# Layer 0's attention: two of three conditioning vectors as running sums on VectorE instead of products on TensorE

## The chip, the cores and the metric

The kernel runs on one core of a Trainium2 chip. The metric is the device time of one execution in microseconds (us), lower is better. TensorE (PE) multiplies, VectorE (DVE), ScalarE (ACT) and GpSimd (POOL) work element by element, SyncE (SP) issues the transfers from memory. Each engine runs its own instructions in the order in which they were written into its queue, and waits for the others through semaphores.

## The reference

A two-layer encoder over 512 positions of width 1024. Layer 0 mixes with pooling and attention, layer 1 with a matrix memory, and each layer ends with a gated channel mixer. Every sub-layer is scaled, shifted and gated by six vectors per layer, all computed from one conditioning vector `c`:

```
cond = jax.nn.silu(c)
for layer in range(DEPTH):
    mod = cond @ ada_w[layer] + ada_b[layer]
    sh1, sc1, g1, sh2, sc2, g2 = jnp.split(mod, 6, axis=-1)
    h = modulate(rms_norm(x), sh1, sc1)
    y = pool_attention_mixer(h, ...)          # layer 0
    x = x + g1[:, None, :] * y
    h = modulate(rms_norm(x), sh2, sc2)
    x = x + g2[:, None, :] * swiglu(h, ...)
```

Each of the six vectors is a product of a row of 1024 numbers with a 1024x1024 matrix: 4 MB of weights for 1024 results. Vectors 0 and 1 (`sh1`, `sc1`) are needed first, vector 2 (`g1`) when the mixer's output is added to `x`, vectors 3 and 4 (`sh2`, `sc2`) for the norm after that.

## The kernel before

Everything is held transposed, features on the 128 partitions and positions along the free dimension. Large products are done in three passes of split float32 (`p_hi*whi`, `p_lo*whi`, `p_hi*wlo`), so each weight slab is cast by ScalarE (`whi`, L116) and its remainder formed by VectorE (`wlo`, L120).

The stage of interest is layer 0's attention, in `even`. It runs `attend` twice, once for each half of the positions (hf 0, then hf 1), 16 units each. A unit is: two products give the scores (`psc`, L840 and L841), VectorE takes the row maximum (`nm`, L843, then a small multiply L846), ScalarE the exponential (`p`, L849), VectorE the reciprocal of its sum (`pr`, L851), GpSimd scales (`p`, L852), TensorE transposes four blocks (`ppt`, L862), ScalarE copies them out (`pt`), and after every second unit TensorE multiplies with the values (`pav`, L874). Between the units of hf 0 stand the last two blocks of the pooling input (`pu`), the four pooling windows (VectorE and GpSimd, `csum`, `win`, `pooled`) and the pooling products (`ppp`). Between those of hf 1 stands the output projection (`pout`, from `project`, woven in at four steps per unit); each of its output tiles is added into `x` by VectorE (`xT`, L332), which also frees the PSUM bank.

Two ways to compute a conditioning vector exist in the code. `ada_pe` streams the weights through TensorE: 16 products of a 32-column stationary with 512 columns per vector (`pada<-araw,silc`, four per tile of 1 MB), then a copy, four transposes (L84) and two small VectorE instructions (L279, L281). `ada` lets VectorE sum them: one scaled copy (`aacc<-araw,silc`, L245) and seven multiply-adds over 128x1024 (L247), a 32x32 block transpose in place (L253), a reduction (L255), four tiny products (`pada<-apart,fold`, L259) and one add (L262). Both read the same tiles `araw` through the same two buffers. Before the change, vectors 2, 3 and 4 of layer 0 go through `ada_pe` during hf 0, and the other seven through `ada` during the channel mixer of layer 0.

From this stage on, the order on each engine is not the order of the code: the compiler's scheduler places instructions by its own estimate of when each could run. The order is fixed in the program; at run time each engine follows its own.

Of the kernel before, what the change touches and what calls it, by code (L numbers as in the profile page):

```python
# [40 lines left out]
def weave(main, *others):  # L41

    for _ in main:
        for g, n in others:
            for _ in range(n):
                if next(g, StopIteration) is StopIteration:
                    break


def drain(g):  # L50
    for _ in g:
        pass


class Trunk:
# [502 lines left out]
    def even(self):  # L558
        nc, a, tc = self.nc, self.a, self.tc
        with ExitStack() as es:  # L560
            at = self.open(es, "at", 1)
            self.qst = self.b.tile([P, KD, S], F32R, name="qst", tag="B_hi")
            kv = self.b.tile([P, KD, S], F32R, name="kvst", tag="B_lo")
            self.kst = kv[:, 0:4]
            self.vst = at.tile([P, NTB, P], F32, name="vst")
            pooled = at.tile([P, 4, S], F32, name="pooled")
            self.edge = at.tile([P, 4, 16], F32, name="edge")
            nc.scalar.dma_start(self.edge, a["k_edge"].partition_broadcast(P))
            self.win = at.tile([P, S], F32, name="win")
            self.csum = at.tile([P, 529], F32, name="csum")  # L570
            nc.gpsimd.memset(self.csum[:, 0:9], 0.0)
            self.rq = [at.tile([P, 2 * NTB], F32, name=f"rq{b}") for b in range(4)]
            slab = None

            def u_block(g):
                nonlocal slab
                if g % 2 == 0:
                    slab = self.next_slab()
                ps = self.bank("pu")
                yield from self.gemm(ps, slab, g % 2, self.h, slice(0, S))  # L580
                if g % 2 == 1:
                    self.free_slabs()
                nc.scalar.copy(pooled[:, g], ps)

            with ExitStack() as es2:
                nt = self.open(es2, "nt", 1)
                self.rope = nt.tile([P, 2, S], F32, name="rope")
                self.load(self.rope, a["k_rope"])
                ada = self.ada_pe(2, 3, 4)
                next(ada)  # L590
                swap = nt.tile([P, P], F32, name="swap")
                i4, s4 = (t.rearrange("p (d t) -> p d t", t=2) for t in (self.ident, swap))
                for e in range(2):
                    nc.gpsimd.tensor_copy(s4[:, :, e:e + 1], i4[:, :, 1 - e:2 - e])
                us = (x for g in range(2) for x in u_block(g))

                def fill(n):
                    for _ in range(n):
                        next(us, None)

                k, v = self.rope_k(nt, swap), self.take_v(nt)
                q = [self.rope_q(nt, swap, b) for b in range(4)]
                for g, n in ((k, 1), (v, 1), (q[0], 1), (v, 1), (k, 1), (q[1], 1), (q[0], 2), (q[2], 2), (q[1], 2),
                             (q[3], 2), (q[2], 2), (q[3], 0)):
                    next(g)
                    fill(n)
                drain(us)
            self.chained = False
            self.mix = self.pair(self.keep, "A")
            self.banks(1)  # L610
            slabs = [None] * 4
            acc = self.square_sums("sqm")
            aw = self.open(es, "aw", 2)
            with tc.issue_after(self.split_ins.ins):
                pool = self.pool_project(pooled)
                next(pool)
                rest = (s for g in (2, 3) for s in u_block(g))
                for i, _ in enumerate(self.attend(aw, 0)):
                    with self.behind(self.sc_ins):
                        for _ in range(2 - i % 2):  # L620
                            next(rest, None)
                        if i < 16:
                            next(ada, None)
                    if i == 11:
                        drain(rest)
                        self.want(*[(a["w_eo"][s], "v") for s in (0, 1, 2, 3, 0)])
                        self.live = 1
                        self.load_slabs()
                    if i in WINDOW_STEPS:
                        with tc.issue_after(self.p_ins.ins), tc.issue_after(self.nm_ins.ins):  # L630
                            self.pool_window(WINDOW_STEPS.index(i), pooled)
                    if i >= POOL_STEP and i % 2 == 0:
                        next(pool, None)
                drain(pool)
            proj = self.project(0, slabs, range(4), self.mix, KD, 0, 2, acc[0])
            drain(ada)
            weave(self.attend(aw, 1), (proj, 4))
            drain(proj)
        self.ffn_want(0)
        self.h2 = self.pair(self.b, "B")  # L640
        self.close(0, slabs, self.mix, KD, 0, 2, acc, 3, self.h2)
        self.banks(0)
# [737 lines left out]
```

## Time and profile before

| | |
|---|---|
| time, median of 3 runs | 1214.58 us (1214.17 to 1219.38) |
| time of the profiled execution | 1214.87 us |
| its span, first to last instruction | 1213.1 us |
| TensorE busy | 1195.9 us, 99% of the span |
| VectorE busy | 656.3 us, 54% |
| ScalarE busy | 476.4 us, 39% |
| GpSimd busy | 135.2 us, 11% |
| mean granted TensorE clock | 0.999 |

Matmuls overlap one another, so a busy TensorE says that it had work, not that it ran at its peak. The chain of waits, followed back from the last instruction, is 92% TensorE.

### The profile page before, as it was taken

The numbers are of one execution on the slowest core, as the hardware profiler recorded it, in microseconds if no ns is written. First come the engines' busy times: TensorE is split into PE (matmuls) and PEld (weight loads), VectorE is DVE, ScalarE is ACT, GpSimd is POOL, SyncE is SP. The second block draws the span as 40 slices with busy tenths as digits, with TensorE's granted clock in tenths as the row PEclk, the third lists the DMA queues.
The fourth block names the chain that finished last, engine by engine and source line by source line (L and its number), as shares of the span: only waits on it lengthen the run. The fifth ranks groups of instructions, "written<-read, shape, count | busy, mean of one in ns | idle before, by whom it ended". The sixth has DMA issues, their size and how long they took to land.

```text
span 1213.1 us, 17266 instructions
## 1 busy us (share of the span) xinstructions
PE 1195.9 (99%) x6930; PEld 1020.9 (84%) x6930; DVE 656.3 (54%) x1111; ACT 476.4 (39%) x902; POOL 135.2 (11%) x151
## 2 busy tenths in 40 slices
PE   8999999999999999999899999999999999999998
PEld 6676689988888888889898999999888888888888
DVE  4576865574865677225878857556523323242233
ACT  4465764433213222223567757534423113221221
POOL 0033220011001110100000101100111001100110
PEclk9999999999999999999999999999999999999999
DMA  9605712274754565222624111113233223232232
GB/s 387 234 29 215 245 51 70 71 277 160 290 209 166 216 242 214 100 79 88 217 70 140 43 63 60 46 59 114 76 101 111 98 87 122 70 106 102 78 96 79
DMA packets 43168, 160.18 MB, mean 132 GB/s; under 512 B 4560, under 2 KB 11344, under 8 KB 36944
## 3 DMA queue, kind: packets, MB, share of 16 engines
q1 hardware_dynamic: 42240, 158.75, 37.2%
q8 instruction: 54, 0.88, 0.3%
q10 hardware_dynamic: 848, 0.33, 0.1%
q14 instruction: 26, 0.21, 0.1%
HBM read 154.87 MB, written 4.19 MB: 131 GB/s over the span
## 4 chain that ended last, share of the span: by engine, by line
PE 92%; DMA 3%; DVE 3%; ACT 1%; issue 1%; POOL 0%; SPq 0%; DVEq 0%; ACTq 0%; POOLq 0%
PE pf L78 53%; PE pout L78 10%; PE po L78 4%; PE pqk L78 3%; PE ppv L1210 3%; PE pv L78 3%; PE z L78 3%; PE pu L78 2%; DMA wraw<-in_w_dram 2%; PE pav L874 2%; PE pada L78 2%; PE ppt L862 1%; DMA wraw<-in_w_od_dram 1%; DVE wlo L120 1%; PE psc L840 1%
## 5 line engine op out<-in xcount | busy, mean ns | idle before, releaser
L78 PE MATMUL pf<-p_lo,whi 128*128 128x512 f32 (+1 forms) x1024 | 383.4, 376 | 0.9 <-DVE p_lo L366 0.9
L78 PE MATMUL pf<-p_hi,wlo 128*128 128x512 f32 (+1 forms) x1024 | 383.0, 376 | 0.0
L78 PE MATMUL pf<-p_hi,whi 128*128 128x512 f32 (+1 forms) x1024 | 380.8, 377 | 1.5 <-ACT p_hi L365 1.5
L116 ACT CAST whi<-wraw 128x1024 fp32r<-128x1024 f32 (+1 forms) x193 | 190.6, 1028 | 335.0 <-PE pf L78 234.8
L120 DVE TENSOR_TENSOR wlo<-wraw,whi 128x1024 fp32r<-128x1024 f32 (+1 forms) x193 | 229.7, 1223 | 137.8 <-ACT whi L116 134.8
L78 PEld LDWEIGHTS pf<-p_lo,whi 128*128 128x128 f32 x1024 | 192.7, 188 | 35.9 <-DVE p_lo L366 1.1
L78 PEld LDWEIGHTS pf<-p_hi,wlo 128*128 128x128 f32 x1024 | 192.5, 188 | 34.9
L78 PEld LDWEIGHTS pf<-p_hi,whi 128*128 128x128 f32 x1024 | 191.0, 188 | 36.6 <-ACT p_hi L365 1.9
L120 POOL TENSOR_TENSOR p_lo<-gf,p_hi 128x512 fp32r<-128x512 f32 (+1 forms) x48 | 70.6, 1474 | 580.3 <-ACT p_hi L116 580.3
L674 DVE TENSOR_TENSOR gf<-pf,si 128x512 f32<-128x512 f32 (+1 forms) x48 | 31.1, 647 | 161.2 <-PE pf L78 144.8
L78 PE MATMUL pout<-p_hi,whi 128*128 128x256 f32 x320 | 91.5, 287 | 0.3 <-DVE xT L332 0.3
L78 PE MATMUL pout<-p_lo,whi 128*128 128x256 f32 x320 | 90.8, 284 | 0.0
L78 PE MATMUL pout<-p_hi,wlo 128*128 128x256 f32 x320 | 90.1, 284 | 0.0
L247 DVE SCALAR_TENSOR_TENSOR aacc<-araw,silc,aacc 128x1024 f32<-128x1024 f32 x49 | 66.1, 1350 | 19.0 <-DMA araw<-in_ada_r_dram 18.0
L116 ACT CAST p_hi<-gf 128x512 fp32r<-128x512 f32 (+1 forms) x48 | 27.9, 581 | 116.7 <-DVE gf L674 116.7
L78 PEld LDWEIGHTS pout<-p_hi,whi 128*128 128x128 f32 x320 | 61.1, 191 | 3.0 <-issue 1.5
L78 PEld LDWEIGHTS pout<-p_lo,whi 128*128 128x128 f32 x320 | 61.3, 191 | 0.4
L78 PEld LDWEIGHTS pout<-p_hi,wlo 128*128 128x128 f32 x320 | 61.0, 191 | 0.4
L672 ACT ACTIVATE si<-pf 128x512 f32<-128x512 f32 (+1 forms) x48 | 26.7, 558 | 76.5 <-PE pf L78 76.5
L717 DVE SCALAR_TENSOR_TENSOR xT<-pf,mod,xT 128x512 f32<-128x512 f32 x32 | 23.9, 748 | 57.2 <-PE pf L78 57.1
L78 PE MATMUL pout<-unit,whi 128*128 128x256 f32 x256 | 47.4, 286 | 0.7 <-ACT unit L1245 0.7
L332 DVE SCALAR_TENSOR_TENSOR xT<-pout,mod,xT 128x256 f32<-128x256 f32 x64 | 28.8, 480 | 31.1 <-PE pout L78 30.9
(248 smaller groups left out, 1730.2 us busy)
## 6 DMA issues: line engine op xcount, KB each, us to landing
wraw<-in_w_dram SPq DMA_DIRECT2D x130, 512.0 KB, 4.5
araw<-in_ada_r_dram SPq DMA_DIRECT2D x40, 1024.0 KB, 6.3
wraw<-in_w_od_dram SPq DMA_DIRECT2D x24, 512.0 KB, 4.6
araw<-in_ada_a_dram SPq DMA_DIRECT2D x8, 1024.0 KB, 15.8
wraw<-in_w_eo_dram SPq DMA_DIRECT2D x10, 512.0 KB, 4.7
wraw<-in_w_oo_dram SPq DMA_DIRECT2D x10, 512.0 KB, 4.5
wraw<-in_w_qkv_dram SPq DMA_DIRECT2D x6, 512.0 KB, 15.3
wraw<-in_w_dram SPq DMA_DIRECT2D x10, 256.0 KB, 2.7
```

Of the source, the lines that this page charges most:

```text
L78: self.pe_last = self.nc.tensor.matmul(*args, **k)
L116: nc.scalar.copy(hi, src)
L120: eng.tensor_tensor(lo, src, hi.bitcast(F32), op=ALU.subtract)
L247: nc.vector.scalar_tensor_tensor(acc, src, s, acc, op0=ALU.mult, op1=ALU.add)
L332: nc.vector.scalar_tensor_tensor(xs, ps, self.mcol(layer, vec, m), xs, op0=ALU.mult, op1=ALU.add)
L672: nc.scalar.activation(si[:, :n], p1, AF.Silu)
L674: ins = nc.vector.tensor_tensor(gf[:, :n], p3, si[:, :n], op=ALU.mult)
L717: nc.vector.scalar_tensor_tensor(self.xT[:, m], ps, self.mcol(layer, 5, m), self.xT[:, m], op0=ALU.mult, op1=ALU.add)
L840: nc.tensor.matmul(ps, lhsT=self.qst[:, h, qs], rhs=self.kst[:, 2 * kv], start=True, stop=False)
L862: nc.tensor.transpose(pt[:, j * P:(j + 1) * P], p[:, j * P:(j + 1) * P], self.ident)
L874: nc.tensor.matmul(po[c, 0:HS], lhsT=self.vst[:, k, c], rhs=pt_of[pr, j][:, k], start=(k == 0), stop=(k == 3), tile_position=(0, 64 * j))
L1210: nc.tensor.matmul(ps[:, d], lhsT=wt[h, d][:, where(d, sb, tb)], rhs=vx[:, sb, h % 2], start=(n == 0), stop=(n == len(seq) - 1))
```

## The change

Vectors 3 and 4 move from `ada_pe` to `ada`. `ada_pe` keeps vector 2. When it is exhausted (after the fifth unit of hf 0), the same variable is pointed at the generator `late`, which issues one step of `ada` behind each further unit of hf 0, and what is left of it one step behind each unit of hf 1. The four products, the transposes and the copies of two vectors go; two sets of VectorE instructions come.

```
-                ada = self.ada_pe(2, 3, 4)
+                ada = self.ada_pe(2)
                 next(ada)
...
             acc = self.square_sums("sqm")
+            late = self.ada((0, 3), (0, 4))
             aw = self.open(es, "aw", 2)
...
                     with self.behind(self.sc_ins):
                         for _ in range(2 - i % 2):
                             next(rest, None)
-                        if i < 16:
-                            next(ada, None)
+                        if next(ada, self) is self:
+                            ada = late
...
             proj = self.project(0, slabs, range(4), self.mix, KD, 0, 2, acc[0])
-            drain(ada)
-            weave(self.attend(aw, 1), (proj, 4))
+            weave(self.attend(aw, 1), (proj, 4), (ada, 1))
             drain(proj)
```

On VectorE the two orders are the same up to L279 and L281, which finish vector 2. The difference from there begins so (- before, + changed; `nm`, `pr` and `csum` as above):

```order
 L279 TENSOR_REDUCE ared<-pada 128x8
+L245 TENSOR_SCALAR aacc<-araw,silc 128x1024
 L281 TENSOR_TENSOR mod<-ared,cols 128x8
-L843 TENSOR_REDUCE nm<-psc 128x1
+L247 SCALAR_TENSOR_TENSOR aacc<-araw,silc,aacc 128x1024
+L843 TENSOR_REDUCE nm<-psc 128x1
+L247 SCALAR_TENSOR_TENSOR aacc<-araw,silc,aacc 128x1024
 L846 TENSOR_TENSOR nm<-nm,rq_522 128x1
 L843 TENSOR_REDUCE nm<-psc 128x1
-L851 RECIPROCAL pr<-psm 128x1
+L247 SCALAR_TENSOR_TENSOR aacc<-araw,silc,aacc 128x1024
```

The sums stand between a unit's maximum, its multiply and its reciprocal, and so on for both vectors. The piece ends where VectorE adds the first finished tiles of the output projection into `xT`. Before, its last rows on VectorE are:

```order
L846 TENSOR_TENSOR nm<-nm,rq_522 128x1
L851 RECIPROCAL pr<-psm 128x1
L843 TENSOR_REDUCE nm<-psc 128x1
L332 SCALAR_TENSOR_TENSOR xT<-pout,mod,xT 128x256 x2
```

In the changed kernel, the transpose and the reduction of the second vector stand ahead of the same row:

```order
L253 STREAM_TRANSPOSE aacc<-aacc 128x1024
L851 RECIPROCAL pr<-psm 128x1
L255 TENSOR_REDUCE apart<-aacc 128x32
L851 RECIPROCAL pr<-psm 128x1
L843 TENSOR_REDUCE nm<-psc 128x1
L846 TENSOR_TENSOR nm<-nm,rq_522 128x1
L851 RECIPROCAL pr<-psm 128x1
L843 TENSOR_REDUCE nm<-psc 128x1
L332 SCALAR_TENSOR_TENSOR xT<-pout,mod,xT 128x256 x2
```

Between L279 and this row VectorE has, before, 17 maxima; changed, 16 maxima and all of the added rows: 2 of L245, 14 of L247, 2 of L253, 2 of L255, 1 of L262 (the second L262 stands a few rows behind), and two pairs of L279 and L281 fewer.

On TensorE, products of the conditioning stood between the units in the second half of hf 0. Before, one such piece reads (`ppp` is a pooling product):

```order
L78 MATMUL pada<-araw,silc 32x512 x4
L862 MATMUL ppt<-ident,p 128x128 x4
L840 MATMUL psc<-kvst,qst 128x512
L841 MATMUL psc<-kvst,qst 128x512
L78 MATMUL ppp<-whi 128x512
```

Changed, the same part of hf 0 has nothing between the units but the pooling products:

```order
L840 MATMUL psc<-kvst,qst 128x512
L841 MATMUL psc<-kvst,qst 128x512
L862 MATMUL ppt<-ident,p 128x128 x8
L874 MATMUL pav<-pt_1043,vst 64x256
L78 MATMUL ppp<-whi 128x512
L78 MATMUL ppp<-wlo,whi 128x512
L78 MATMUL ppp<-whi,wlo 128x512
```

The transposes now stand in pairs of units, each of which needs two units' `p`. From the 97th product of `pout` (the first of its second group, which needs the banks that the `xT` rows free) to the first product of the channel mixer (`pf`), TensorE has the same rows in both kernels, but for one unit's score pair and four transposes more in the changed one; after that the same instructions to the end.

## Rows read from the trace of the kernel before

**Rows 1.** The page: busy time of TensorE, share of the span, instructions.
```profile
PE 1195.9 (99%) x6930; PEld 1020.9 (84%) x6930; DVE 656.3 (54%) x1111; ACT 476.4 (39%) x902; POOL 135.2 (11%) x151
```

**Rows 2.** Busy time in two stretches; columns PE, PEld, DVE, ACT, POOL, clock, DMA.
```profile
103.20:156.84 53.64, 53.31 (x355) 36.21 (x356) 35.25 (x82) 34.34 (x69) 13.91 (x23) 1.00 0.60 207
156.84:192.00 35.16, 35.16 (x262) 29.16 (x259) 17.76 (x47) 18.87 (x43) 7.43 (x11) 1.00 0.09 31
```

**Rows 3.** Chain of waits, 100 to 135 us: start, length, what.
```profile
107.41 1.85 PE pada L78 x16
...
115.21 0.99 PE pada L78 x8
...
124.19 0.44 PE pada L84 x4
```

**Rows 4.** VectorE in order of time, both ends of the stretch: start, length.
```profile
103.31 0.18 DVE L279 TENSOR_REDUCE ared<-pada 128x8 f32<-128x16 f32 x1 [0.56 <-PE pada L84]
...
156.23 0.69 DVE L843 TENSOR_REDUCE nm<-psc 128x1 f32<-128x512 f32 x1
156.84 0.87 DVE L332 SCALAR_TENSOR_TENSOR xT<-pout,mod,xT 128x256 f32<-128x256 f32 x2
```

**Rows 5.** Groups on VectorE, 103.2 to 156.84 us: busy us, mean ns, idle before.
```profile
L843 DVE TENSOR_REDUCE nm<-psc 128x1 f32<-128x512 f32 x17 | 11.6, 687 | 7.8 <-PE psc L841 7.7
...
L851 DVE RECIPROCAL pr<-psm 128x1 f32<-128x1 f32 x16 | 2.4, 157 | 5.1 <-ACT p L849 5.0
```

**Rows 6.** VectorE in order of time, `ada` during the channel mixer.
```profile
249.28 0.75 DVE L245 TENSOR_SCALAR aacc<-araw,silc 128x1024 f32<-128x1024 f32 x1 [0.39 <-DMA araw<-in_ada_r_dram]
...
269.94 1.25 DVE L253 STREAM_TRANSPOSE aacc<-aacc 128x1024 f32<-128x1024 f32 x1
271.22 1.22 DVE L255 TENSOR_REDUCE apart<-aacc 128x32 f32<-128x1024 f32 x1
272.36 0.68 DVE L674 TENSOR_TENSOR gf<-pf,si 128x512 f32<-128x512 f32 x1
...
286.29 1.28 DVE L247 SCALAR_TENSOR_TENSOR aacc<-araw,silc,aacc 128x1024 f32<-128x1024 f32 x1
287.50 0.16 DVE L262 TENSOR_TENSOR mod<-pada,cols 128x8 f32<-128x8 f32 x1
```

**Rows 7.** Groups, 84 to 500 us, and durations (minimum, median, maximum) of L852.
```profile
L247 DVE SCALAR_TENSOR_TENSOR aacc<-araw,silc,aacc 128x1024 f32<-128x1024 f32 x49 | 66.1, 1350 | 19.0 <-DMA araw<-in_ada_r_dram 18.0
L245 DVE TENSOR_SCALAR aacc<-araw,silc 128x1024 f32<-128x1024 f32 x7 | 8.0, 1142 | 0.7 <-DMA araw<-in_ada_r_dram 0.7
...
L852 POOL TENSOR_SCALAR p<-p,pr x32: 691/692/1588, 88.7 to 182.8; 128x512 f32<-128x512 f32 x32
```

**Rows 8.** Busy time in the two fullest stretches of VectorE; columns as in rows 2.
```profile
130.00:140.00 10.00, 9.67 (x63) 6.26 (x62) 9.31 (x21) 7.57 (x14) 3.21 (x5) 1.00 0.64 228
140.00:150.00 10.00, 10.00 (x79) 8.82 (x79) 8.45 (x15) 8.00 (x15) 1.79 (x3) 1.00 0.69 211
```

**Rows 9.** Chain of waits, then TensorE in order of time.
```profile
156.66 1.87 PE pav L874 x14
...
159.72 0.23 PE psc L840
...
160.18 0.44 PE ppt L862 x4
...
160.37 0.36 PE L78 MATMUL pout<-p_hi,whi 128*128 128x256 f32 x1
...
286.62 0.25 PE L259 MATMUL pada<-apart,fold 128*32 128x8 f32 x8
```

**Rows 10.** Busy time and granted clock early on; columns as in rows 2.
```profile
10.00:15.00 5.00, 4.15 (x35) 2.62 (x33) 2.79 (x5) 1.72 (x4) 1.02 (x1) 0.80 1.01 419
...
50.00:55.00 5.00, 3.15 (x14) 2.28 (x13) 4.54 (x7) 3.23 (x4) 0.00 (x0) 1.00 1.01 401
```

**Rows 11.** Transfers issued from 84 to 165 us: count, size, median us to landing.
```profile
araw<-in_ada_r_dram SPq DMA_DIRECT2D x10, 1024.0 KB, 4.9
```

More of the change, by code (lines that the diff above doesn't have):

```diff
@@ L588, in even @@
                 self.load(self.rope, a["k_rope"])
-                ada = self.ada_pe(2, 3, 4)
+                ada = self.ada_pe(2)
                 next(ada)
@@ L612, in even @@
             acc = self.square_sums("sqm")
+            late = self.ada((0, 3), (0, 4))
             aw = self.open(es, "aw", 2)
@@ L621, in even @@
                             next(rest, None)
-                        if i < 16:
-                            next(ada, None)
+                        if next(ada, self) is self:
+                            ada = late
                     if i == 11:
@@ L635, in even @@
             proj = self.project(0, slabs, range(4), self.mix, KD, 0, 2, acc[0])
-            drain(ada)
-            weave(self.attend(aw, 1), (proj, 4))
+            weave(self.attend(aw, 1), (proj, 4), (ada, 1))
             drain(proj)
```

## The prediction

> **What bounds the kernel now.** I read the busy times first. TensorE is busy 99% of the span and VectorE 54% [rows 1]. Taken over the whole kernel, moving work from TensorE to VectorE looks like a pure gain, so the next thing to read is the stage where the work lands. The piece that matters begins where VectorE finishes vector 2 (L279, at 103.31 us) and ends where it adds the first tiles of the output projection into `xT` (L332, at 156.84 us) [rows 4]. Both kernels have the same orders up to the first of these, so 103.3 us stands in both. In this piece of 53.64 us TensorE is busy 53.31 us and VectorE 35.25 us; in the 35 us behind it TensorE is busy all of 35.16 us and VectorE half of it [rows 2]. Before the change the piece is therefore TensorE's: of VectorE's 18.4 idle us most lie ahead of a maximum that waits for the scores (7.8 us) and ahead of a reciprocal that waits for the exponential (5.1 us) [rows 5].
>
> **What the change takes from TensorE.** Eight tiles of products and two sets of transposes. On the chain of waits two tiles together take 1.85 us, each of five more 0.99 us (115.21 us is the first of them), and each set of transposes 0.44 us [rows 3]. The eighth tile, at 133.5 us, lies under a wait of other engines and is off the chain. That is 1.85 + 5 x 0.99 + 2 x 0.44 = 7.7 us, and 8.7 us if the eighth counts. What comes is two sets of four tiny products, 0.25 us a set [rows 9]. So TensorE could give back about 8.5 us, and its work in the piece falls to about 45 us.
>
> **What it gives to VectorE.** Neighbouring instructions overlap a little, so I count from start to start. The scaled copy takes 0.75 us, a multiply-add 1.21 us (286.29 to 287.50), the transpose 1.28 us and the reduction 1.14 us [rows 6]. Ahead of the first `xT` row the new order has both vectors entire: 2 x 0.75 + 14 x 1.21 + 2 x 1.28 + 2 x 1.14 + 0.1 = 23.4 us. Gone from the piece are two pairs of L279 and L281, 0.18 us for such a row [rows 4], and one unit's maximum, multiply and reciprocal (0.69 us, and two of about 0.16 us [rows 5]): 1.6 us together. VectorE's bare work in the piece becomes 35.25 + 23.4 - 1.6 = 57.1 us. That is more than the 53.64 us which the whole piece takes now, and far more than TensorE's 45 us. VectorE takes its instructions strictly in order, so the `xT` row cannot start before 103.3 + 57.1 = 160.4 us, 3.6 us later than now. The point at which the change would start to cost is 45 - 33.7 = 11 us of added VectorE work; it adds 23.4.
>
> **What comes on top of the bare sum.** First, collisions with GpSimd. The multiply-add has a mean of 1350 ns, the scaled copy one of 1142 ns [rows 7], against 1.28 and 0.75 us undisturbed [rows 6]: 14 x 0.07 + 2 x 0.39 = 1.7 us. Below it the bound is nothing, since those means come from the channel mixer, where GpSimd does other work. GpSimd's scaling of `p` shows the same from its side: 692 ns as a rule, up to 1588 ns [rows 7].
>
> The Trainium skill's page "SBUF — State Buffer" ("Who interferes with whom") speaks harder against this change: a VectorE instruction with two inputs in SBUF and a GpSimd instruction that reads SBUF exclude each other, and the later one waits in full. By it, if each of the 16 scalings in the piece held VectorE up for its whole 0.69 us, the 1.7 us would be 11 us and the forecast below 1232 us. The rows have seldom a full collision, so the sum goes by them.
>
> Second, waits that VectorE still has. The low bound is none, if something in its queue is always ready. The high bound is its share in the fuller windows now: busy 8.45 of 10 us from 140 us on [rows 8] would make 58.8 us of work take 69.6 us; with 9.31 of 10, as from 130 us on, 63.2 us. I take 2.5 us. In the new order some 3 us of other VectorE work stand between a unit's multiply and its reciprocal, longer than the exponential needs, so the waits of [rows 5] are mostly filled. Four places remain where nothing covers it: the first maximum behind a pair of transposes that need two units' `p`, and the last two units ahead of `xT`, which have no sums between them, with the last products of the first group behind them.
>
> **Transfers.** The eight tiles are the same 1 MB tiles as before, through the same two buffers; only who frees a buffer changes. A tile lands 4.9 us after its issue [rows 11], and VectorE now uses one per 7 us, so I cost them at nothing. What hides them is the other VectorE work between the sums; without this cover a multiply-add waits as in the channel mixer, 19.0 us over 49 [rows 7], which for 14 is 5.4 us. On SP's queue all ten `w_eo` weight loads stood behind the eight tiles; now the first four, which the first group of `pout` needs, stand behind four of them, two behind seven, and the last four, not needed before the piece ends, behind all.
>
> **The sum.** VectorE ends the piece after 57.1 + 1.7 + 2.5 = 61.3 us, at 164.6 us instead of 156.84: +7.8 us. Now `pout`'s second group starts at 160.37 us [rows 9], 3.5 us behind the `xT` row. In the new order one score pair, the tiny products, a set of value products and one of transposes stand between, 0.46 + 0.25 + 1.87 + 0.44 = 3.0 us by [rows 9]: 0.5 us less. From there on TensorE is full now [rows 2], and has one unit's scores and transposes more to do, 0.46 + 0.44 = +0.9 us. Together +8.2 us. The 8.5 us that leave TensorE are not in this sum: they turn into idle time of TensorE while it waits for `p`. The profiled execution took 1214.87 us (its span 1213.1), 0.3 us over the median of 1214.58. Predicted: 1214.87 + 8.2 = 1223.1 us. With no collisions and no waits it is 3.6 - 0.5 + 0.9 = +4.0, 1218.9 us; with the waits of the 140 us window 16.1 - 0.5 + 0.9 = +16.5, 1231.4 us.
>
> **The rivals.** About 0.5% (6 us) is what a measurement of this kernel can tell from no change.
>
> *TensorE's time comes back* (faster, chance 0.09). 1214.87 - 8.5 = 1206.4 us. For it speaks that TensorE is the busy engine all through, and that VectorE idles 18.4 us in the piece. It needs VectorE's added work under 11 us ahead of the `xT` row, so it would take multiply-adds of half their measured length, or scores that run on without the maxima behind the sums; the order excludes the latter.
>
> *The delay is made up behind the piece* (no change, 0.06). If TensorE's second group did not hang on the `xT` row, only the 0.9 us would remain: 1215.8 us. Against it stand the banks, which that row frees, and a TensorE without idle time from 156.84 us on [rows 2].
>
> *TensorE's clock falls* (slower still, 0.07). TensorE will have work for some 45 of 61 us. With 4.15 of 5 us busy the granted clock was 0.80, early in the kernel, but with 3.15 of 5 it was 1.00 [rows 10]. If ten of these microseconds ran at 1.2 instead of 2.4 GHz, 5 us of products would be added, of which the idle time covers part: up to 1228 us. The Trainium skill's page "TensorE: Matmul & The Clock Gate" ("HAM oscillation — how this bites in real kernels") has this as its rule for bursts of matmuls with waits between them; the rows show both outcomes.
>
> The forecast itself, VectorE as the bound of the piece, has 0.78. It covers 1218.9 to 1231.4 us, and about a fifth of it (0.16) lies under +0.5%.
>
> **How the numbers follow.** Range 1216 to 1231: the low end takes in most of "made up behind" and all of the bare sum, the high end the waits of the fuller window and the clock; the faster rival and a remainder above stay out. The likeliest case's own range is 1219 to 1231. Faster by over 0.5%: 0.09. Within 0.5%: 0.16 + 0.06 = 0.22. Slower by over 0.5%: 0.62 + 0.07 = 0.69.
>
> **What would show it.** In the profile after: VectorE busy over 90% from 103 us to the first `xT` row, and that row near 164.6 us; L247 there near 1.3 us; TensorE with some 10 us or more of idle time in the piece, waiting for GpSimd's `p` or for the exponential; the first `pf` some 8 us later than now, and from there on the same distance to the end. The prediction is wrong if the `xT` row comes before 160 us, if VectorE waits there for `araw` transfers or weights by more than a few us, or if the orders behind the piece lose or win time of their own.

## The result and the profile after

| | before | after |
|---|---|---|
| median of 6 runs each, in turn | 1217.54 us | 1225.59 us (predicted 1223.1, range 1216 to 1231) |
| profiled execution | 1214.87 us | 1222.41 us |
| its span | 1213.1 us | 1220.6 us |

The ratio of the times is 1.0069, with a 95% interval of 1.0054 to 1.0085: slower by 0.7%, some 8 us. One of the six executions after was a slow one of 5275.65 us; it counts in the median of the table but not in the ratio, and the median of the other five is 1224.43 us. Timed again beside three experiments, the changed kernel gave 1.0071 (1.0053 to 1.0089).

The busy times of the whole, and the shares of the chain of waits (the chain followed back from the last instruction), after:

```profile
PE 1191.0 (98%) x6874; PEld 1018.8 (83%) x6874; DVE 676.0 (55%) x1129; ACT 476.2 (39%) x900; POOL 139.8 (11%) x151
...
PE 88%; DVE 6%; DMA 3%; issue 2%; ACT 1%; POOL 0%; ACTq 0%; DVEq 0%; POOLq 0%
```

Against [rows 1] TensorE has 4.9 us less to do, VectorE 19.7 us more. The piece from L279 (102.72 us) to the first `xT` row (161.73 us) is cut out in the first row; the second and third rows cut it in two at the first product of `pout`, the fourth is the 35 us behind it, the last three look into its worst place:

```profile
core 0: us, PE busy (x) PEld busy (x) DVE busy (x) ACT busy (x) POOL busy (x), PEclk, DMA share, GB/s
102.72:161.73 59.01, 47.95 (x288) 34.63 (x288) 55.05 (x96) 32.88 (x63) 18.37 (x22) 0.94 0.52 188
102.72:130.72 28.00, 20.98 (x109) 13.67 (x109) 27.45 (x45) 16.26 (x30) 6.80 (x10) 0.88 0.62 226
130.72:161.73 31.01, 26.97 (x186) 20.96 (x180) 27.60 (x52) 16.62 (x34) 11.56 (x13) 1.00 0.44 153
161.73:197.00 35.27, 35.27 (x267) 29.39 (x266) 18.46 (x51) 19.45 (x45) 7.65 (x11) 1.00 0.09 31
120.00:125.00 5.00, 2.19 (x7) 0.82 (x6) 5.00 (x8) 2.88 (x5) 0.00 (x0) 0.89 0.58 180
125.00:130.00 5.00, 2.79 (x8) 2.21 (x9) 5.00 (x9) 2.15 (x4) 0.69 (x1) 0.50 0.82 346
130.00:135.00 5.00, 5.00 (x42) 3.59 (x41) 5.00 (x13) 2.41 (x5) 2.47 (x2) 0.93 0.00 0
```

Beside [rows 2] the engines have changed places: VectorE is busy 55.05 of 59.01 us (93%), TensorE idles 11.06 us. Before, the piece took 156.84 - 103.31 = 53.53 us [rows 4], so it is longer by 59.01 - 53.53 = 5.5 us. The idle time is not spread evenly: between 120 and 130 us TensorE works 4.98 of 10 us, and the granted clock falls to 0.50, the lower of its two levels.

What TensorE waits for in the piece, by the view of waits (total us, times, longest):

```profile
PE psc L840 <- ACT p L849: 4.2, 3, 3.3
PE ppt L862 <- POOL p L852: 2.0, 3, 1.0
PE ppp L78 <- DVE pooled L824: 1.6, 1, 1.6
```

The longest of them in VectorE's timeline (start, us):

```profile
120.66 0.68 DVE L843 TENSOR_REDUCE nm<-psc 128x1 f32<-128x512 f32 x1
121.26 0.80 DVE L824 TENSOR_SCALAR pooled<-ppp,cols 128x512 f32<-128x512 f32 x1
...
122.05 1.21 DVE L120 TENSOR_TENSOR wlo<-wraw,whi 128x1024 fp32r<-128x1024 f32 x1
123.18 0.68 DVE L120 TENSOR_TENSOR wlo<-pooled,whi 128x512 fp32r<-128x512 f32 x1
123.78 1.23 DVE L253 STREAM_TRANSPOSE aacc<-aacc 128x1024 f32<-128x1024 f32 x1
124.94 1.18 DVE L120 TENSOR_TENSOR wlo<-wraw,whi 128x1024 fp32r<-128x1024 f32 x1
126.05 0.14 DVE L846 TENSOR_TENSOR nm<-nm,rq 128x1 f32<-128x1 f32 x1
```

and in TensorE's:

```profile
127.21 0.79 PE L840 MATMUL psc<-kvst,qst 128*128 128x512 f32 x1 [3.33 <-ACT p L849]
127.80 0.63 PE L841 MATMUL psc<-kvst,qst 128*128 128x512 f32 x1
```

A unit's maximum ends at 121.34 us. Its small multiply, 0.14 us of work, stands behind five larger rows and starts at 126.05 us. ScalarE's exponential (`p`), which empties the bank for the next scores, needs it. But the multiply isn't all that the exponential waited for. Ahead of it in ScalarE's queue stands the cast of a weight slab, which had waited for its transfer; the third line is SyncE's longest wait in the two us from 119 us on (total us, times, longest):

```profile
125.26 1.04 ACT L116 CAST whi<-wraw 128x1024 fp32r<-128x1024 f32 x1 [1.37 <-DMA wraw<-in_w_eo_dram]
126.29 0.78 ACT L849 ACTIVATE p<-psc,nm,rq 128x512 f32<-128x512 f32 x1
...
SPq L89 <- DVE wlo L120: 4.6, 1, 4.6
```

This transfer was issued at 120.77 us, when VectorE's split of an earlier slab (`wlo`, 119.53 to 120.74 us) had freed its buffer, and the cast ended at 126.30 us. With the multiply in time, the exponential would by this order still have started near 126.3 us. Both ways lead through VectorE's full row, which never pauses here. The scores that come at 127.21 us take 0.79 and 0.63 us, against 0.50 and 0.40 us at 123.14 and 123.48 us, before the clock fell.

From the `xT` row on the distance grows a little more: the second group of `pout` starts at 165.21 us (before 160.37), the first `pf` at 218.93 us (before 212.32), and the span ends 7.5 us later, of which one us is lost near 590 us in layer 1.

### The profile page after: what moved, and what is told of

Read it like the earlier page. It is cut to its first block, busy times and chain, and to the rows that moved or that the text cites. A ratio compares the mean times of both kernels' runs of the same rounds, so it can differ in the third digit from the quotient of the medians.

```text
span 1220.6 us, 17171 instructions
## 1 busy us (share of the span) xinstructions
PE 1191.0 (98%) x6874; PEld 1018.8 (83%) x6874; DVE 676.0 (55%) x1129; ACT 476.2 (39%) x900; POOL 139.8 (11%) x151
## 4 chain that ended last, share of the span: by engine, by line
PE 88%; DVE 6%; DMA 3%; issue 2%; ACT 1%; POOL 0%; ACTq 0%; DVEq 0%; POOLq 0%
PE pf L78 53%; PE pout L78 10%; PE po L78 4%; PE pqk L78 3%; PE ppv L1210 3%; PE pv L78 3%; PE z L78 3%; PE pu L78 2%; DVE wlo L120 2%; DMA wraw<-in_w_od_dram 1%; PE pav L874 1%; DVE aacc L247 1%; DMA wraw<-in_w_dram 1%; PE pada L78 1%; PE ppt L862 1%
## 5 line engine op out<-in xcount | busy, mean ns | idle before, releaser
L247 DVE SCALAR_TENSOR_TENSOR aacc<-araw,silc,aacc 128x1024 f32<-128x1024 f32 x63 | 84.3, 1338 | 17.9 <-DMA araw<-in_ada_r_dram 16.8
L717 DVE SCALAR_TENSOR_TENSOR xT<-pf,mod,xT 128x512 f32<-128x512 f32 x32 | 23.9, 747 | 57.2 <-PE pf L78 57.1
```

The source lines that it names most:

```text
L247: nc.vector.scalar_tensor_tensor(acc, src, s, acc, op0=ALU.mult, op1=ALU.add)
L717: nc.vector.scalar_tensor_tensor(self.xT[:, m], ps, self.mcol(layer, 5, m), self.xT[:, m], op0=ALU.mult, op1=ALU.add)
```

## The experiments

Each kernel was timed in turn with the kernel before. "The piece" is always L279 of vector 2 to the first `xT` row.

**Sums without their work.** The sums run over 8 of 1024 columns, with nothing folded, so that vectors 3 and 4 hold other numbers.

```
+                self.ada_accumulate(acc[:, 0:8], t2[:, k % 2, 0:8], k)
...
+            nc.vector.tensor_tensor(self.mod[:, c], acc[:, 0:8], self.adab[:, c], op=ALU.add)
...
-            late = self.ada((0, 3), (0, 4))
+            late = self.ada_thin((0, 3), (0, 4))
```

> The sums of vectors 3 and 4 are made over 8 of the 1024 columns of each tile, with no transpose, no reduction and no fold behind them (this leaves out 1016 columns of each sum, so the two vectors hold other numbers); every transfer is kept with its place. Theory 1 (VectorE's work bounds the piece): about 20 us of VectorE work goes from the piece, TensorE with some 45 to 48 us is the bound again, the piece takes 47 to 50 us and the time is 1206 to 1211 us, faster than the kernel before. Rival A (TensorE without filler products loses the time in waits for scores and exponentials): 1216 to 1222 us with TensorE idle over 6 us in the piece. Rival B (transfers): 1222 to 1227 us.

Measured 1213.69 us, ratio 0.9975 (0.9963 to 0.9987). Its piece, and ten us of it:

```profile
104.86:155.69 50.83, 47.73 (x284) 35.30 (x286) 37.97 (x95) 33.25 (x66) 13.85 (x23) 0.93 0.60 218
...
120.00:125.00 5.00, 3.27 (x11) 2.08 (x12) 5.00 (x8) 5.00 (x9) 0.00 (x0) 0.81 0.97 374
125.00:130.00 5.00, 5.00 (x19) 2.40 (x18) 4.18 (x10) 1.33 (x4) 1.52 (x3) 0.51 0.45 139
```

VectorE's work is the cause: without it the changed order and the same transfers end before the old kernel. But the time lies above theory 1's 1206 to 1211 us. TensorE still idles 3.1 us, most of it from 120 to 125 us, where VectorE is full without the sums too, and the 8 us of products taken from TensorE are worth only some 3 us.

**Sums and products together.** For each tile the four products are issued as well, into a bank that nobody reads.

```
+                    for q in range(4):
+                        self.ada_products(ps, q, k + q % 2, t2[:, q % 2, (q // 2) * 512:(q // 2) * 512 + 512], k == 0, k == 6)
                 self.ada_accumulate(acc, t2[:, k % 2], k)
```

> The sums stay on VectorE as in the changed kernel, and as many products as each tile had before go through TensorE as well, into a bank that nobody reads (work added that the result doesn't need). Theory 1 (VectorE bounds the piece, TensorE idles about 11 us in it): the products fill idle time of TensorE, the piece stays at 58 to 62 us and the time at 1222 to 1230 us; TensorE idles some 3 to 5 us in place of 11. Rival A (the loss came of TensorE running out of filler or of its clock falling after idle): the time comes back towards that of the kernel before, 1214 to 1219 us. Rival C (both engines are at their limit): the 7 to 8 us of products come on top, 1230 to 1235 us.

Measured 1229.15 us, ratio 1.0101 (1.0082 to 1.0121). Its piece:

```profile
105.05:166.62 61.57, 54.33 (x341) 34.69 (x342) 55.22 (x93) 31.30 (x60) 15.20 (x21) 0.94 0.51 180
```

The filler brings nothing back, which refutes rival A. It isn't free either: TensorE has 6.4 us more work in the piece than in the changed kernel, the piece is 2.6 us longer, 7.2 us of TensorE's time stay idle where theory 1 said 3 to 5. Rival C's 1230 us lies inside the interval; against it stands that 3.9 us came on top of the changed kernel's time, with an uncertainty of some 3 us, and not 7 to 8. The four kernels make a table, as ratios to the kernel before:

| | sums left out or thin | sums on VectorE | the sums cost |
|---|---|---|---|
| products on TensorE | 1 | 1.0101 | 1.0%, 12.3 us |
| no products | 0.9975 | 1.0069 | 0.9%, 11.4 us |
| the products cost | 0.25%, 3.0 us | 0.3%, 3.9 us | |

(1% is 12.2 us. The intervals of two ratios leave their difference uncertain by some 0.25%; the 3.0 us, read from one ratio, lie between 1.6 and 4.5.) The changed kernel pays 11 to 12 us for the sums and gets 3 to 4 back for the products. Each of the four was laid in an order of its own, and the kernel with both has the products without their transposes and copies, so these are prices of the work together with the order that came with it.

**Vector 4 alone on VectorE**, in the first half.

```
-                ada = self.ada_pe(2)
+                ada = self.ada_pe(2, 3)
...
-            late = self.ada((0, 3), (0, 4))
+            late = self.ada((0, 4))
```

> Vector 3 goes back to products on TensorE, only vector 4 is summed on VectorE. Theory 1 (the piece from L279 to the first xT is bound by VectorE's row of instructions in order, about 57 us of work there in the changed kernel): the piece loses about 11 us of VectorE work and gets some 4 us of TensorE work back, so both engines end near 46 to 49 us and the piece falls to about 52 to 54 us, the time to 1210 to 1217 us, within 0.5% of the kernel before. Rival A (the work on VectorE isn't the cause; the sums as such disturb the order of TensorE's rows, its filler products being gone): half of the filler is back, half of the loss of 8 us stays, about 1219 to 1222 us. Rival B (the transfers of the conditioning tiles and of the weights behind them decide): these keep their order, so the time stays at 1222 to 1227 us.

Measured 1235.99 us, ratio 1.0156 (1.0133 to 1.0179): half the sums, and ten us slower than with both. All three expectations failed. The piece, three parts of it, and the ten us before the last of them:

```profile
104.90:176.43 71.53, 60.19 (x343) 38.82 (x344) 46.22 (x93) 35.65 (x71) 19.27 (x24) 0.88 0.44 155
104.90:125.50 20.60, 20.60 (x129) 12.31 (x129) 9.73 (x27) 10.83 (x24) 5.84 (x10) 1.00 0.60 216
125.50:164.90 39.40, 28.06 (x121) 14.98 (x119) 35.90 (x66) 23.82 (x46) 13.43 (x14) 0.78 0.47 168
164.90:176.43 11.53, 11.53 (x104) 11.53 (x97) 0.59 (x2) 1.01 (x3) 0.00 (x0) 1.00 0.01 1
...
155.00:160.00 5.00, 4.21 (x13) 2.49 (x13) 5.00 (x10) 2.25 (x6) 1.39 (x2) 0.50 0.67 210
160.00:165.00 5.00, 5.00 (x27) 2.44 (x25) 1.40 (x7) 2.38 (x6) 2.08 (x3) 0.53 0.01 5
```

VectorE has 46.22 us of work in 71.53 us, so VectorE's total alone doesn't bound it. The engines take turns: first TensorE is full (vector 3's products) with VectorE half idle, then VectorE is full with TensorE at 28 of 39 us and a mean clock of 0.78, and last TensorE does the first group of `pout` in one lump, with VectorE idle. In this kernel's order that group comes after 24 units; in the changed kernel it begins after 15.

**Vector 4's sums behind the request for the `w_eo` weights.** As the last kernel, but `late` starts after unit 11; the first `pout` products come after 14 units.

```
-                        if next(ada, self) is self:
+                        if i < 8 or i > 11:
+                            next(ada, None)
+                        if i == 11:
+                            drain(ada)
+                            ada = late
```

> Vector 4 alone on VectorE, in the first half as in the run of 1236 us, but from the twelfth unit on, behind the request for the output projection's weights, so that on SP's queue these weights stand ahead of vector 4's tiles and the first products of the output projection come after 14 units in place of 24. The bare VectorE work ahead of the first xT is the same. Theory 2 (the 1236 us came of an order in which TensorE had nothing but scores and transposes while VectorE was full, with the projection's products in one lump behind it): the time falls by 10 us or more, to 1218 to 1226 us, and no slow-clock stretch behind 150 us. Rival (VectorE's load from 125 to 160 us as such): 1232 to 1238 us.

Measured 1222.73 us, ratio 1.0047 (1.0032 to 1.0062). Its piece:

```profile
103.38:157.57 54.19, 48.59 (x305) 33.17 (x306) 43.83 (x84) 30.93 (x61) 15.16 (x21) 1.00 0.57 204
```

Much the same VectorE work, 17 us less piece, clock at 1.00 throughout: the 1236 us were the order's doing. The edit moves instructions and transfers together; which of the two orders did it wasn't separated, but in the kernel of 1236 us no wait of TensorE from 95 to 235 us is put down to a transfer (ScalarE waited 3.4 us for these weights).

**Vector 4's sums behind the piece.** Vector 3 as products; vector 4's sums wait for the eighth unit of hf 1. Against the kernel before, without the lines of the helper `gated`, which lets eight units pass:

```
-                ada = self.ada_pe(2, 3, 4)
+                ada = self.ada_pe(2, 3)
...
+            later = self.ada((0, 4))
...
-            weave(self.attend(aw, 1), (proj, 4))
+            weave(self.attend(aw, 1), (proj, 4), (self.gated(later, 8), 1))
```

> One vector on VectorE again, as in the run with vector 4 alone (1236 us), but its sums are moved to the units of the second half from its eighth on, behind the stretch from 125 to 160 us in which that run had VectorE full and TensorE at 28 of 39 us; the first group of the output projection is issued after 14 units and not after 24. Theory 2 (a stretch is bound by the fuller of the two engines in that stretch, and what is moved costs nothing only where the other engine is the fuller one and its own work stands ready): 3 multiply-adds stay ahead of the first xT, TensorE loses one vector's 4 us of products, VectorE has about half of its time free behind; the time is 1211 to 1217 us. Theory 1 in its bare form (the sum of VectorE's work from L279 to xT decides) says about the same here, 1210 to 1216 us, but it can't tell why the earlier run took 1236 us with 46 us of VectorE work in the piece. Rival (sums on VectorE are dear wherever they stand): 1222 us and more.

Measured 1215.15 us, ratio 0.9990 (0.9976 to 1.0005): no difference from the kernel before. The piece and what follows it, in an execution of 1220.17 us, the longest of the twelve:

```profile
105.02:156.67 51.65, 50.06 (x327) 35.61 (x328) 37.52 (x83) 33.63 (x67) 13.39 (x22) 1.00 0.50 173
156.67:192.00 35.33, 34.81 (x259) 28.43 (x255) 24.19 (x56) 18.47 (x42) 7.19 (x11) 1.00 0.25 92
```

Behind the piece VectorE carries 24.19 us in place of 17.76 [rows 2] and TensorE still works 34.81 of 35.33 us: here one vector's sums are hidden.

**Vector 3 in the first half, vector 4 in the second**, from its eighth unit; both on VectorE.

```
-            late = self.ada((0, 3), (0, 4))
+            late, later = self.ada((0, 3)), self.ada((0, 4))
...
-            weave(self.attend(aw, 1), (proj, 4), (ada, 1))
+            drain(ada)
+            weave(self.attend(aw, 1), (proj, 4), (self.gated(later, 8), 1))
```

> The sums of vector 3 stay behind the first half's scores, those of vector 4 are moved to the units of the second half from its eighth on, most of them behind the piece. Theory 1: about 7 to 8 us of VectorE work leaves the piece (10 multiply-adds and one transpose with its reduction stay), VectorE's work there is near 50 us, that of TensorE near 46 to 49 us; behind the piece VectorE had about half of its time free, so nothing is given back there: the time is 1211 to 1217 us. Rival A (TensorE without filler): 1219 to 1225 us. Rival D (the sums are as dear behind the piece as in it): as the changed kernel, 1222 to 1228 us.

Measured 1223.81 us, ratio 1.0057 (1.0039 to 1.0075); theory 1's 1211 to 1217 us failed. The ranges of rival A and of rival D both hold it, and by its ratio it can't be told from the changed kernel (1.0069). Against rival D stands the kernel above, in which the same sums at the same place had no net cost; against rival A, that TensorE's filler brought nothing back. The piece, cut at the first product of `pout`:

```profile
104.62:161.76 57.14, 48.20 (x299) 36.05 (x301) 49.04 (x90) 34.01 (x65) 17.33 (x22) 0.94 0.49 166
104.62:132.60 27.98, 20.97 (x108) 13.67 (x108) 27.43 (x45) 16.23 (x30) 6.78 (x10) 0.89 0.58 191
132.60:161.76 29.16, 27.23 (x199) 22.38 (x193) 21.61 (x46) 17.78 (x36) 10.55 (x13) 0.99 0.40 142
```

The first part equals that of the changed kernel, 28 us, with VectorE full. In the second VectorE has 6.0 us less to do (21.61 against 27.60) and the part is shorter by 1.9 us: TensorE has work for 27.23 of its 29.16 us and is the fuller engine now. What was won there is too little for the time to show.

**Both vectors' sums with the second half.**

```
-                        if next(ada, self) is self:
-                            ada = late
+                        next(ada, None)
...
-            weave(self.attend(aw, 1), (proj, 4), (ada, 1))
+            weave(self.attend(aw, 1), (proj, 4), (self.gated(late), 1))
```

> Both vectors' sums are issued with the units of the second half only; the scheduler still puts 10 multiply-adds ahead of the first xT, late in the piece, where the other work of VectorE from 120 to 140 us (splits of weights, the pooled branch) is over. Theory 2 (what counts is where the sums lie): TensorE's stretch of waits from 120 to 130 us shrinks to that of the run with thin sums (3 us idle in the piece), then VectorE is full up to 180 us, more than it has free there (17 us of 35): 1215 to 1221 us. Theory 1 in its bare form, 10 multiply-adds less the rest: 1211 to 1215 us. Rival (sums dear everywhere): 1224 us or more.

Measured 1219.89 us, ratio 1.0036 (1.0024 to 1.0047), inside theory 2's range. Its details came out only in part. The piece is short, 51.29 us, but TensorE idles 5.8 us in it, where 3 were expected: the waits moved with the sums, to 130 to 145 us. Behind it VectorE is busy 24.87 of 35.18 us, so not full, and TensorE works 32.29 us:

```profile
103.53:154.82 51.29, 45.52 (x289) 33.48 (x286) 45.86 (x87) 31.15 (x63) 17.97 (x22) 1.00 0.53 185
...
130.00:145.00 15.00, 10.21 (x65) 7.27 (x64) 15.00 (x26) 8.47 (x16) 4.44 (x5) 1.00 0.58 202
154.82:190.00 35.18, 32.29 (x222) 26.17 (x218) 24.87 (x59) 18.55 (x43) 8.70 (x11) 0.90 0.21 76
```

**The small multiply on GpSimd**, in the changed kernel and, as controls, in the kernel before and in the kernel with vector 4 behind the piece.

```
-            self.nm_ins = nc.vector.tensor_tensor(nm, nm, rq, op=ALU.mult)
+            self.nm_ins = nc.gpsimd.tensor_tensor(nm, nm, rq, op=ALU.mult)
```

> The changed kernel with each unit's small multiply (L846, 128x1) moved from VectorE to GpSimd, in both layers. In the changed kernel this multiply stood up to 5 us behind its maximum in VectorE's row, with weight splits and a transpose between, and TensorE waited 3.3 us for that unit's exponential. Theory 1 (VectorE's throughput): some 16 x 0.1 us leave VectorE in the piece, GpSimd adds a hand-over to each unit; 1221 to 1228 us, VectorE over 90% busy in the piece as before. Rival (latency: the loss comes of the place of the multiply in VectorE's row): TensorE's longest wait for p falls under 1.5 us, the piece shrinks by 3 us or more, 1216 to 1221 us.

> The kernel before, with each unit's small multiply (L846) moved from VectorE to GpSimd. It is the control for the changed kernel with that move, which took 5.5 us less than the changed kernel. If the move pays where VectorE is crowded (theory: the multiply's place in VectorE's row, between sums, held scores up), it brings nothing here, where VectorE has 18 idle us in the piece: 1214 to 1219 us. Rival (the move pays by itself, or through another order of the units): 1209 to 1213 us.

> Vector 3 as products, vector 4's sums behind the eighth unit of the second half (the run of 1215.2 us), and the small multiply on GpSimd as well. If both are independent and the second pays only where VectorE is crowded: 1211 to 1215 us, possibly faster than both kernels. If the hand-over to GpSimd costs each unit some time where nothing else waits: 1215 to 1220 us.

Measured, in this order: 1220.16 us, ratio 1.0025 (1.0014 to 1.0036); 1217.56 us, 1.0012 (1.0003 to 1.0021); 1221.20 us, 1.0036 (1.0024 to 1.0049). The piece of the first:

```profile
105.70:162.21 56.51, 50.55 (x312) 36.70 (x311) 53.01 (x82) 35.24 (x69) 33.42 (x40) 0.94 0.55 196
```

In the changed kernel the move brings 0.45%, five to six us, within the rival's range; in the kernel before it brings nothing. So of these three kernels it paid only in the one with a crowded VectorE. Whether by the place of the multiply or by the amount of work isn't settled: TensorE's longest wait for the exponential is 1.7 us in place of 3.3, but VectorE's busy time in the piece also fell by 2.5 us against the changed kernel run beside it (55.54 us), which is most of the 3.0 us by which the piece is shorter (59.50 us there). The other 2.3 us come behind the piece, where VectorE isn't full (first `pf` 111.4 us after L279, there 116.7), and the scheduler laid the units in another order too. The third kernel lost 0.46% by the same move, and came out above both of its expectations; its piece is hardly longer than without the move (51.97 and 51.65 us), TensorE waits 2.4 us for VectorE's `sqm` at 220.8 us, and the rest of its loss is open.

**The changed kernel again**, beside the first of these, the one with vector 4 behind the piece and the one behind the weights.

> The changed kernel itself, timed beside the three others on the same chip. Expected as measured: 1222 to 1228 us, ratio 1.0054 to 1.0085, piece from L279 to xT near 59 us. If it were 2 us or more away from that, differences of a few us between runs of different calls could not be read.

Measured 1225.69 us, ratio 1.0071; the piece is 59.50 us.

## Why the prediction was right, and where its steps were not

**What bounds the piece: shown, with a limit.** VectorE's load is the cause: thin sums take the loss away with every transfer kept, added products don't. VectorE was busy over 90%, as said, and waited for no transfer there. TensorE idled 11.06 us, as said (10 or more), 6.2 of them waiting for the exponential and for `p`. The limit is the order: it changes with every edit, and between two kernels with the same sums (vector 4 alone, and behind the weights) it was worth 13 us.

**The size of the piece: too large by 2.3 us.** Predicted +7.8 us, measured +5.5. Bare work was put at 57.1 us; VectorE's busy time, collisions included, is 55.05. The added rows were rightly priced: from start to start they take 23.7 us, put at 23.4. What was missed is that the old rows move together too: a VectorE row starts some 0.07 us before the one ahead of it ends. In the piece the durations of the timeline's rows add up to 39.24 us over 78 rows before, for 35.25 us busy, 0.05 us a row; and to 61.73 us over 94 rows after, for 55.05 us, 0.07 us a row. Collisions were put at 1.7 us; L247 and L245 of VectorE and L852 of GpSimd in the piece, after, in the views of these lines (min/median/max in ns):

```profile
L247 DVE SCALAR_TENSOR_TENSOR aacc<-araw,silc,aacc x14: 1260/1276/1423, 103.6 to 153.2; 128x1024 f32<-128x1024 f32 x14
...
L245 DVE TENSOR_SCALAR aacc<-araw,silc x2: 736/744/753, 102.8 to 133.5; 128x1024 f32<-128x1024 f32 x2
...
L852 POOL TENSOR_SCALAR p<-p,pr x16: 688/692/2167, 102.3 to 160.8; 128x512 f32<-128x512 f32 x16
```

The multiply-add's median is the undisturbed 1.28 us of [rows 6], its maximum 0.14 us more, so none of the sums waited for a scaling's 0.69 us. The collisions fell on GpSimd, whose scaling of `p` went up to 2167 ns. The longest one, beside VectorE's two rows of that time, each with two inputs in SBUF:

```profile
134.58 2.17 POOL L852 TENSOR_SCALAR p<-p,pr 128x512 f32<-128x512 f32 x1 [1.86 <-DVE nm L846]
...
134.39 0.68 DVE L825 TENSOR_TENSOR p_lo<-pooled,p_hi 128x512 fp32r<-128x512 f32 x1
135.00 1.27 DVE L247 SCALAR_TENSOR_TENSOR aacc<-araw,silc,aacc 128x1024 f32<-128x1024 f32 x1
```

The Trainium skill's page "SBUF — State Buffer" ("Who interferes with whom") says that the order of issue decides which of the two waits. The first row agrees with that: it began 0.19 us ahead of the scaling. The second doesn't, by the starts in the profile, of which GpSimd's are rough: the multiply-add began 0.42 us behind the scaling, took its undisturbed 1.27 us, and the scaling ended only 0.5 us behind it. So in a full row of VectorE it was GpSimd that went on waiting. Waits of VectorE were put at 2.5 us; they were 59.01 - 55.05 = 3.96. Two of the prediction's sums are off without bearing on its time: sixteen full collisions would by its figures give 1232.4 us, not below 1232, and 8.7 us of products and transposes less 0.5 us of tiny products leave 8.2, not 8.5.

**"VectorE ends the piece": wrong in its last ten us.** The last stretch of the chain of waits ahead of that row belongs to TensorE:

```profile
149.85 1.20 DVE aacc L247
151.05 0.61 DVE p_lo L825
151.71 3.27 PE pout L78 x25
154.97 0.44 PE ppt L862 x4
```

From 105 to 151.7 us nearly all of the chain is VectorE's, with 2.2 us of GpSimd; the ten us from there to the row are TensorE's. So VectorE bounds most of the piece, not its end. The experiments show the same: with vector 4 moved away the first part stays at 28.0 us, and in the second TensorE is the fuller engine.

**"The 8.5 us that leave TensorE are not in this sum: they turn into idle time of TensorE": wrong, by how much is uncertain.** With the sums on VectorE their removal is worth 3.9 us by the table, some 3 us either way; with thin sums 3.0 us. That TensorE is the fuller engine in other stretches of the same piece (above) would account for it; this is argued. TensorE's busy time in the piece fell to 47.95 us, not to 45. Before this gain the sums cost 11 to 12 us, not the 8.2 of the sum. So the time came out right in part by luck: a cost and a gain that were both put too low cancelled.

**"11 us of added VectorE work" as the point of decision: refuted.** It was the difference of two totals. One vector's sums, by the prediction's prices 0.75 + 7 x 1.21 + 1.28 + 1.14 = 11.6 us, cost 0.47% behind the weights, 1.56% at their worst place, and nothing behind the piece. With vector 3's products still on TensorE the same reckoning puts the point some 4 us higher, near 15 us, so the first two should have been free as well.

**Behind the piece: +2.3 us more than said.** Predicted +0.4 (-0.5 and +0.9). The second group of `pout` comes 3.48 us behind the `xT` row, before 3.53: the -0.5 did not come. Up to the first `pf` TensorE is busy 1.2 us longer, with one more unit's scores and transposes, as said, and the tiny products of the second vector, and has 0.5 us more idle time. The last us, in layer 1, wasn't foreseen. So 5.5 in the piece, 1.7 up to `pf` and one in layer 1, less 0.6 us by which this execution was ahead at L279, make the 7.5 us between the two spans: near +8.2, by a term that was too large and one that was too small. The prediction had named time lost behind the piece as a sign of being wrong; 2.7 us were lost there, 0.4 of them foreseen.

**The rivals.** TensorE's time came back in part (above), but not so as to make the kernel faster. The delay was not made up behind: 57.20 us from the `xT` row to `pf` in place of 55.48. TensorE's clock did fall, from 125 to 130 us; in the changed kernel it fell where VectorE was full and on the chain of waits, so it should have cost little. What the time would have been without the fall wasn't measured.

## What to carry to other kernels

Moving work to an engine with idle time must be judged stretch by stretch: the totals of a piece said 11 us were free, yet half of the sums cost from nothing to 19 us, depending on where they stood. Look for the stretch in which the receiving engine is already full before the change (here from 130 to 140 us, [rows 8]) and put the work past it; even there only one of the two vectors was free. A small instruction that another engine waits for stands behind every large one in a full row (here 4.7 us for one of 0.14), and so does a row that frees a buffer for the next transfer. A right time can hide two wrong terms: the pair of experiments "new work without its weight" and "new work with the old kept" separates cost from gain, as far as the order stays alike.

No version here that computes both vectors beats the kernel before by more than its measurement can tell: the best, with vector 4 behind the piece, is its equal.

## What the runs showed of the hardware that was not expected

Which waits lower TensorE's clock could not be foretold from [rows 10], and the new rows, five us each, don't sort by busy time either. In the changed kernel 2.19 of 5 us busy stood at 0.89 and the next five at 0.50. With thin sums 3.27 of 5 us stood at 0.81 and the next five at 0.51, although TensorE was busy in all of them. With both vectors in the second half 2.89 of 5 us, from 130 us on, stood at 1.00, and so did the next five. With vector 4 behind the weights 3.53 of 5 us, from 120 us on, and all that follow in the piece stood at 1.00. With vector 4 alone the low level (0.53) lasted from 160 to 165 us, where TensorE had work in all five, so that there a fall can cost time; in the changed kernel it lay where TensorE had work for 2.79 of 5 us.

Of a VectorE row and a GpSimd row that both read SBUF, the one that began later didn't always wait: the scaling that began at 134.58 us took 2.17 us, the multiply-add that began at 135.00 us its usual 1.27 us.
